# Splitting the output projection's weights and one group of down-projection weights ahead of their use in a hybrid decoder block

## The chip, the cores and the metric

One core of one Trainium2 chip runs the whole kernel. The metric is the device time of one execution in microseconds (us). The profile describes one execution by its span, from the first instruction to the end of the last; the time of that execution is a little longer than its span.

## What is computed

One decoder layer on a sequence of 2048 tokens with 1024 features, all in float32. An RMS norm, a combined input projection, two mixing branches (stick-breaking attention over 8 heads, chunked gated linear attention over 4 heads), an output projection with residual, a second norm, a convolutional feed-forward part with residual, and a last norm:

```python
h = rms_norm(x, attn_norm_g[l])
proj = h @ w_in[l]
...
x = x + jnp.concatenate([o_sb, o_gla], axis=-1) @ w_out[l]
h = rms_norm(x, ffn_norm_g[l])
u = causal_depthwise_conv(h @ w_ffn_up[l], conv_w[l], conv_b[l])
a, val = jnp.split(u, 2, axis=-1)
x = x + (jax.nn.silu(a) * val) @ w_ffn_down[l]
return rms_norm(x, final_norm_g)
```

`w_out` is 1024 x 1024, `w_ffn_down` is 2816 x 1024.

## The kernel before

**Split products.** Every large product is made of three matmuls. Each operand is split into a rounded high part and the remainder, and hi\*hi, hi\*lo and lo\*hi are added up in PSUM (lines 759 to 761 for the output and the down-projection). So each weight tile has to be split before it is used: `split_w` (line 101) copies it on ScalarE into the high part (L102) and subtracts on GpSimd, in a few places on VectorE, for the low part (L103). The 2048 tokens are worked on in four blocks of 512, and every block needs the same weights. Block 0 loads a weight raw (256 KB for 128 rows by 512 columns), splits it, uses it, and writes the split pair (512 KB) to a DRAM tile (`wou` for `w_out`, `wdn` for `w_ffn_down`, `wup` for the up-projection). Blocks 1 to 3 load the split pair. That choice stands in `load` (lines 741 to 752).

**Stages.** First, `prep` (line 193) normalises and transposes x, and `gv_block` (line 183) makes the values of the gated branch from it, 16 tiles of 128 tokens, in about 116 us. Then come the low-rank gate and the gated branch's queries and keys (lines 243 to 295), to about 220 us; the attention's Q, K and V projections together with the chunked linear attention (lines 416 to 430); the output gate together with the attention of block 0 (lines 650 to 679); and then, from about 680 us, four times `ffn` (line 812). `ffn` is the output projection (`accumulate`, line 728, once for each half n of the columns), the transposes, and three groups of 8, 7 and 7 chunks of up-projection, each followed by its share of the down-projection (`accumulate` again). The attention of blocks 1 to 3 is woven into the `ffn` stages.

**Buffers around the change.** `load_chunk` (line 148) loads the input projection's weights through the two `raw` buffers (line 125) and splits them into four `w` buffers. `m1` (line 128) is one buffer: it holds `gat` (the norm's gain) in the first stage, then `gvr` (the gated branch's values, line 300), and from line 708 on the split pair `d2`. In block 0 `accumulate` uses, for the first half of the output projection, raw tiles in slot 11 and four split pairs in slots 10 and 14 (`ahead`, lines 676 to 682); for everything else two raw tiles (`drr`) and a ring `dr` of three split pairs (lines 707 to 710). More pairs join `dr` only later (lines 724 to 725 and 926).

**What sets the order.** The program is unrolled. When it is built, a planner gives every engine and every DMA queue its order: it goes through the program with a timeline of its own, and lets an instruction that is ready by that timeline run ahead of earlier ones that are not (`schedule_with_timeline_sim=True`, line 992). On the chip each engine then runs its list in that order and waits on semaphores. From line 626 on TensorE alone keeps the order in which the program was written (`manual_schedule`). A tile of a pool with one buffer is only given out again when all that used it has finished, DMA included.

Of the kernel before, what the change touches and what calls it, by code (L numbers as in the profile page):

```python
# [8 lines left out]
F32 = mybir.dt.float32  # L9
# [7 lines left out]
P = 128  # L17
# [3 lines left out]
TB = 512  # L21
# [29 lines left out]
def hybrid_block_kernel(ctx, tc, x, attn_norm_g, w_in, w_gate_up, b_gate_up, sb_out_g,  # L51
# [66 lines left out]
    if True:  # L118
# [54 lines left out]
        def mm_tok(w, b, t):  # L173
            ps = mm_ps()
            whi, wlo = w
            ts = slice(t * P, (t + 1) * P)
            for k in range(KT):
                nc.tensor.matmul(ps, hh[b][k // 4][:, k % 4, ts], whi[k], start=(k == 0), stop=False)  # L178
                nc.tensor.matmul(ps, hh[b][k // 4][:, k % 4, ts], wlo[k], start=False, stop=False)  # L179
                nc.tensor.matmul(ps, hl[b][k // 4][:, k % 4, ts], whi[k], start=False, stop=(k == KT - 1))  # L180
            return ps

        def gv_block(w, b):
            for t in range(4):
                ps = mm_tok(w, b, t)
                gt = ev.tile([P, 2, TB], F32, tag="ev", name="gt")[:, 0]
                nc.scalar.activation(gt, ps, AF.Copy)
                nc.sync.dma_start(out=gvs[b][t * P:(t + 1) * P, :], in_=gt)

        with tc.tile_pool(name="xp", bufs=2, side="right") as xp, tc.tile_pool(name="sm", bufs=2, side="right") as sm:  # L190
            gat = m1_tile([P, D], F32, "gat")

            def prep(b):
                for t in range(4):
                    xt = xp.tile([P, D], F32, tag="xt", name="xt")
                    r0 = b * TB + t * P
                    nc.sync.dma_start(out=xt, in_=x[r0:r0 + P, :])
                    if r0 == 0:
                        nc.scalar.dma_start(out=gat, in_=attn_norm_g.to_broadcast([P, D]))
                    xn = xp.tile([P, D], F32, tag="xn", name="xn")  # L200
                    ss = sm.tile([P, 1], F32, tag="ss", name="ss")
                    nc.scalar.activation(xn, xt, AF.Square, accum_out=ss)
                    r = rstd_of(sm, ss, D, 1, "n")
                    nc.vector.scalar_tensor_tensor(out=xn, in0=xt, scalar=r, in1=gat, op0=ALU.mult, op1=ALU.mult)
                    for k4 in range(2):
                        tp = pt.tile([P, 4, P], F32, tag="tp", name="tp")
                        for kk in range(4):
                            k = 4 * k4 + kk
                            nc.tensor.transpose(tp[:, kk, :], xn[:, k * P:(k + 1) * P], ident)
                        dh = hh[b][k4][:, :, t * P:(t + 1) * P]  # L210
                        dl = hl[b][k4][:, :, t * P:(t + 1) * P]
                        split_psum(dh, dl, tp)

            prep(0)
            w = load_chunk(OFF_GV)
            for b in range(NB):
                if b + 1 < NB:
                    prep(b + 1)
                gv_block(w, b)
# [6 lines left out]
        with tc.tile_pool(name="lr", bufs=2, side="right") as lp, tc.tile_pool(name="lc", bufs=1, side="right") as lc:  # L226
# [16 lines left out]
            for b in range(NB):  # L243
                pl = mm_ps()
                for k in range(KT):
# [5 lines left out]
                nc.scalar.activation(lr[64:96, :], pl[0:32, :], AF.Copy)  # L251
                nc.vector.tensor_tensor(out=lr[32:64, :], in0=pl[0:32, :], in1=lr[0:32, :].bitcast(F32),
                                        op=ALU.subtract)
                pq0 = mm_feat(w, b, 0)
                for j in range(NPAIR):
                    pg = mm_ps()
# [397 lines left out]
    for b in range(NB):  # L654
        for t in range(4):
            for part, _ in enumerate(og_group(b, t)):
                if b > 0:

                    if steps < (16 * (b - 1) + 4 * t + part + 1) * FIRST // 46:
                        next(first, None)  # L660
                        steps += 1
                    for f, when in enumerate(PAIRS):
                        if f not in oT and steps >= when:
                            oT[f] = o_feat(0, f, pc, "c")
                for f, row in GATED.items():
                    if f not in oT and (b, t) >= row:
                        oT[f] = o_feat(0, f, pc, "c", ot=ots[f % 4])
            if (b, t) == (1, 3):
                gring.items += gated_rows(0)
                a4 = slot(4, [P, 4, TB], F32, "wtC")  # L670
                w45 = slot(5, [P, 2, 2, TB], F32R, "ws45")
                wsr.items += [w45[:, 0], w45[:, 1]]
                ots = [a4[:, k, :].rearrange("p (t q) -> p t q", t=4) for k in range(4)]
            elif (b, t) == (2, 3):
                gring.items += gated_rows(1)
                wraw = slot(11, [P, 4, TB], F32, "wraw")
                wsplit = slot(10, [P, 4, TB], F32R, "wsplit")
    for _ in first:
        pass
    wmore = slot(14, [P, 4, TB], F32R, "wmore")  # L680
    ahead = [Ring([wraw[:, k, :] for k in range(4)]),
             Ring([m[:, 2 * u:2 * u + 2, :] for m in (wsplit, wmore) for u in range(2)])]
    del wsr.items[2:]
    c1.close()
    rings, o2 = later_memory(*shared[:-1], a4, shared[-1])
# [39 lines left out]
            dr.items += [m[:, 2 * u:2 * u + 2, :] for m in spare for u in range(2)]  # L725
        return True

    def accumulate(lhs, w_rows, kept, b, squares=None, extra=None, stagger=False, rstds=None, rows=None, first=None,
                   final=False):


# [3 lines left out]
        for n in range(2):  # L735
# [4 lines left out]

            def load(ci):
                at_ = kept[n][rows[ci]]
                pair = first[1].next() if n == 0 and first else dr.next()
                if b > 0:
                    nc.sync.dma_start(out=pair.bitcast(F32), in_=at_.bitcast(F32))
                else:
                    raw = first[0].next() if n == 0 and first else drr.next()
                    nc.sync.dma_start(out=raw, in_=w_rows[rows[ci] * P:(rows[ci] + 1) * P, ns])
                    split_w(pair[:, 0, :], pair[:, 1, :], raw, nc.vector if first and n == 0 and ci % 2 else nc.gpsimd)
                    nc.gpsimd.dma_start(out=at_.bitcast(F32), in_=pair.bitcast(F32))  # L750
                whi, wlo = pair[:, 0, :], pair[:, 1, :]
                return whi, wlo
# [59 lines left out]
    def ffn(b, oT, rows, nextT):  # L812
# [15 lines left out]
        if b == 0:  # L828
# [4 lines left out]
        r2 = sm.tile([P, 4], F32, tag="r2", name="r2", bufs=2)  # L833
        rs1, rs2 = ([r[:, t:t + 1] for t in range(4)] for r in (r1, r2))
        last = b + 1 == NB
        yield from accumulate(oT, w_out, wou, b, squares=sq1, stagger=True, rstds=[r1], rows=rows,
                              extra=previous if b > 0 else remaining, first=None if b > 0 else ahead)
        if b == 0:
            h2h.extend(slot(10 + u, [P, 4, TB], F32R, f"h2h{u}") for u in range(2))
# [24 lines left out]
        for gi, G in enumerate(GROUPS):  # L864
# [49 lines left out]
            if final and b + 1 < NB:  # L914
                def extra(n, ci, G):
                    if ci == G - 1 or n == 1:
                        nextT.append(o_feat(b + 1, len(nextT), *((pc, "c") if done == total else (pz, "z"))))
            yield from accumulate(gts, w_ffn_down[ch0 * P:(ch0 + G) * P, :], [w[ch0:ch0 + G] for w in wdn], b, squares=sq2 if final else None,
                                  extra=extra, stagger=final and last, rstds=[r2], final=final and last)
            ch0 += G  # L920
        while b + 1 < NB and len(nextT) < KT:
# [74 lines left out]
```

## Time and profile before

| | us |
|---|---|
| median of 3 runs | 2766.29 |
| lowest and highest run | 2762.18, 2768.05 |
| time of the profiled execution | 2762.93 |
| its span | 2761.2 |

A row of the timeline reads: start and duration in us, engine, line, operation, the tile written and the tiles read, shapes, how many instructions were merged, and in square brackets how long the engine had been idle before and which event ended that idle time. PE is TensorE, DVE VectorE, ACT ScalarE, POOL GpSimd, SP the queue of SyncE; a DMA row gives the time to issue, not to transfer. In a table of windows each engine has its busy time and its count of instructions, followed by the TensorE clock that was granted (1.00 is 2.4 GHz, the lower level is 1.2 GHz, a value between them a mix of the two in time), the busy share of the DMA engines, and GB/s.

### The profile page before, as it was taken

Reading aid. Unit: us, or ns where it says so; the run is one execution under the profiler, and the core shown is the slowest. Engines: PE = TensorE matmul, PEld = TensorE weight load, DVE = VectorE, ACT = ScalarE, POOL = GpSimd, SP = SyncE. Lnnn points to the kernel's source line nnn. Section 1 sums busy time; section 2 is a strip of 40 time slices with the busy share of each in tenths; the row PEclk is TensorE's granted clock in tenths of the full one; section 3 lists DMA queues with packets and bytes.
Section 4 is the critical chain, followed back from the end, with each engine's and each line's share of the span. In section 5 each row is a group of like instructions: output and inputs, shape, how many; then the busy total and the mean of one; then the engine's idle time right before and its main releaser. Section 6 shows DMA issues by size and latency. Waiting matters only on the chain.

```text
span 2761.2 us, 36066 instructions
## 1 busy us (share of the span) xinstructions
PE 2696.3 (98%) x13000; PEld 2235.0 (81%) x13000; DVE 1686.7 (61%) x2777; ACT 1146.3 (42%) x2371; POOL 610.7 (22%) x937
## 2 busy tenths in 40 slices
PE   8999999999899899999999999999999999999998
PEld 7878888878688778887888888888888888888887
DVE  5246755457677687777776877777867334242333
ACT  5455533335465455554543444445434222220112
POOL 2001212214555555543111111111110000000000
PEclk9999999999999999999999999999999999999999
DMA  6215644477667677768455555574554656555552
GB/s 193 91 62 175 231 143 150 126 180 238 237 226 256 223 240 258 241 232 279 156 185 183 177 172 176 185 253 151 179 176 151 232 191 218 206 197 191 198 190 84
DMA packets 254563, 526.92 MB, mean 191 GB/s; under 512 B 54864, under 2 KB 143024, under 8 KB 231856
## 3 DMA queue, kind: packets, MB, share of 16 engines
q1 hardware_dynamic: 223136, 387.76, 42.8%
q0 software_dynamic: 31104, 136.33, 13.7%
q8 instruction: 102, 1.67, 0.2%
q14 instruction: 77, 0.63, 0.1%
q10 hardware_dynamic: 144, 0.52, 0.1%
HBM read 382.99 MB, written 141.56 MB: 190 GB/s over the span
## 4 chain that ended last, share of the span: by engine, by line
PE 85%; DVE 5%; DMA 4%; POOL 2%; ACT 2%; issue 2%; SPq 1%; ACTq 0%; POOLq 0%; DVEq 0%
PE ups L881 11%; PE ups L882 11%; PE ups L883 11%; PE d L760 6%; PE d L759 6%; PE d L761 6%; PE z L533 4%; PE tp L566 4%; PE mm L170 2%; PE mm L169 2%; PE mm L168 2%; PE acc L582 2%; PE mm L179 2%; PE mm L180 2%; PE mm L178 2%; PE acc L581 2%
## 5 line engine op out<-in xcount | busy, mean ns | idle before, releaser
L881 PE MATMUL ups<-h2h,u 128*128 128x512 f32 x1408 | 552.2, 392 | 3.9 <-DVE x L786 3.9
L882 PE MATMUL ups<-h2l,u 128*128 128x512 f32 x1408 | 551.0, 391 | 0.0
L883 PE MATMUL ups<-h2h,u 128*128 128x512 f32 x1408 | 550.3, 391 | 0.0
L881 PEld LDWEIGHTS ups<-h2h,u 128*128 128x128 f32 x1408 | 265.1, 188 | 60.5 <-DVE x L786 4.4
L883 PEld LDWEIGHTS ups<-h2h,u 128*128 128x128 f32 x1408 | 264.9, 188 | 57.2
L95 DVE TENSOR_TENSOR ws<-tp,ws 128x512 fp32r<-128x512 f32 (+1 forms) x320 | 193.8, 606 | 191.9 <-ACT ws L94 191.0
L882 PEld LDWEIGHTS ups<-h2l,u 128*128 128x128 f32 x1408 | 265.0, 188 | 55.5
L759 PE MATMUL d<-d,g 128*128 128x512 f32 x736 | 290.9, 395 | 4.2 <-DVE x L786 1.8
L94 ACT ACTIVATE ws<-tp 128x512 fp32r<-128x512 f32 (+1 forms) x320 | 170.2, 532 | 299.9 <-PE tp L566 295.5
L760 PE MATMUL d<-d,g 128*128 128x512 f32 x736 | 289.3, 393 | 1.5 <-POOL d L103 1.5
L761 PE MATMUL d<-d,g 128*128 128x512 f32 x736 | 288.7, 392 | 0.0
L893 DVE SCALAR_TENSOR_TENSOR ct<-ups,cwb,ct 128x511 f32<-128x511 f32 x176 | 131.7, 748 | 249.2 <-POOL ct L892 196.2
L888 ACT ACTIVATE ct<-ups,cwb 128x512 f32<-128x512 f32 x176 | 136.3, 775 | 340.3 <-PE ups L883 340.1
L549 DVE TENSOR_TENSOR_SCAN wtB<-mt,cy 128x512 f32<-128x512 f32 x192 | 248.4, 1294 | 3.1 <-ACT mt L538 3.0
L786 DVE TENSOR_TENSOR x<-d,x 128x512 f32<-128x512 f32 x128 | 85.8, 683 | 166.1 <-PE d L761 166.0
L892 POOL TENSOR_TENSOR ct<-ct,hadd 128x2 f32<-128x2 f32 x132 | 26.4, 200 | 688.7 <-ACT halo L890 324.5
L538 ACT ACTIVATE mt<-z 128x512 f32<-128x512 f32 (+2 forms) x320 | 170.5, 533 | 9.4 <-DVE cy L553 5.1
L759 PEld LDWEIGHTS d<-d,g 128*128 128x128 f32 x736 | 138.7, 189 | 36.0 <-DVE x L786 3.4
L760 PEld LDWEIGHTS d<-d,g 128*128 128x128 f32 x736 | 138.6, 188 | 31.8 <-POOL d L103 2.5
L761 PEld LDWEIGHTS d<-d,g 128*128 128x128 f32 x736 | 138.5, 188 | 30.9
L168 PE MATMUL mm<-hh,w 128*128 128x512 f32 x384 | 151.2, 394 | 0.0
L170 PE MATMUL mm<-hh,w 128*128 128x512 f32 x384 | 149.4, 392 | 0.8 <-POOL w L103 0.8
(262 smaller groups left out, 5375.4 us busy)
## 6 DMA issues: line engine op xcount, KB each, us to landing
u<-wup SPq DMA_DIRECT2D x132, 1024.0 KB, 4.7
d<-wdn SPq DMA_DIRECT2D x94, 512.0 KB, 3.4
wup<-u POOLq DMA_DIRECT2D x44, 1024.0 KB, 6.6
kvA<-kvs POOLq DMA_DIRECT2D x52, 512.0 KB, 4.8
uraw<-in_w_ffn_up_dram SPq DMA_DIRECT2D x44, 512.0 KB, 4.6
wdn<-d POOLq DMA_DIRECT2D x44, 512.0 KB, 5.2
d<-wou SPq DMA_DIRECT2D x38, 512.0 KB, 4.3
dw<-wdn SPq DMA_DIRECT2D x38, 512.0 KB, 4.2
```

Source lines behind the costliest of these rows:

```text
L94: nc.scalar.activation(hi, ps, AF.Copy)
L95: nc.vector.tensor_tensor(out=lo, in0=ps, in1=hi.bitcast(F32), op=ALU.subtract)
L168: nc.tensor.matmul(ps, whi[k][:, fs], hh[b][k // 4][:, k % 4, :], start=(k == 0), stop=False)
L170: nc.tensor.matmul(ps, wlo[k][:, fs], hh[b][k // 4][:, k % 4, :], start=False, stop=(k == KT - 1))
L538: nc.scalar.activation(m[:, lo:TB], z[:, :width], AF.Sigmoid, scale=-0.125)
L549: nc.vector.tensor_tensor_scan(out=pp[:, ::-1], data0=mr, data1=mr, initial=1.0 if prev is None else prev, op0=ALU.mult, op1=ALU.bypass)
L759: nc.tensor.matmul(accs[t], gh[:, ts], whi, start=(ci == 0), stop=False)
L760: nc.tensor.matmul(accs[t], gh[:, ts], wlo, start=False, stop=False)
L761: nc.tensor.matmul(accs[t], gw[:, ts], whi, start=False, stop=(ci == G - 1))
L881: nc.tensor.matmul(ps, whi[:, k, :], hk, start=(k == 0), stop=False)
L882: nc.tensor.matmul(ps, whi[:, k, :], lk, start=False, stop=False)
L883: nc.tensor.matmul(ps, wlo[:, k, :], hk, start=False, stop=(k == KT - 1))
```

## The change

A new helper loads a raw weight tile, splits it and writes the pair to DRAM. It is called 16 times in the first stage for all of `w_out`, through a pool `sp` with one raw tile and one pair, and 16 times in the second stage (four for each block) for the first 8 chunks of `w_ffn_down`, through the two `raw` buffers and the single `m1` buffer. Block 0 of the output projection, and the first group of block 0's down-projection, then load split pairs as the other blocks do. The first half of the output projection gets eight pairs (slots 10, 11, 14, 15) and needs no raw tiles.

```diff
+        def split_ahead(raw, pair, src, dst):
+            nc.sync.dma_start(out=raw, in_=src)
+            split_w(pair[:, 0, :], pair[:, 1, :], raw)
+            nc.gpsimd.dma_start(out=dst.bitcast(F32), in_=pair.bitcast(F32))
+
         def gv_block(w, b):
             for t in range(4):
+                i = 4 * b + t
+                split_ahead(sp.tile([P, 512], F32, tag="sraw", name="sraw"),
+                            sp.tile([P, 2, 512], F32R, tag="spair", name="spair"),
+                            w_out[(i // 2) * P:(i // 2 + 1) * P, (i % 2) * 512:(i % 2 + 1) * 512], wou[i % 2][i // 2])
                 ps = mm_tok(w, b, t)
...
+                tc.tile_pool(name="sp", bufs=1) as sp:
...
+                for i in range(4 * b, 4 * b + 4):
+                    split_ahead(raw_tile([P, 512], F32, "sraw"), m1_tile([P, 2, 512], F32R, "spair"),
+                                w_ffn_down[(i // 2) * P:(i // 2 + 1) * P, (i % 2) * 512:(i % 2 + 1) * 512],
+                                wdn[i % 2][i // 2])
                 pq0 = mm_feat(w, b, 0)
...
-                wraw = slot(11, [P, 4, TB], F32, "wraw")
-                wsplit = slot(10, [P, 4, TB], F32R, "wsplit")
+                wsplit = [slot(n, [P, 4, TB], F32R, f"ws{n}") for n in (10, 11)]
...
-    wmore = slot(14, [P, 4, TB], F32R, "wmore")
-    ahead = [Ring([wraw[:, k, :] for k in range(4)]),
-             Ring([m[:, 2 * u:2 * u + 2, :] for m in (wsplit, wmore) for u in range(2)])]
+    wsplit += [slot(n, [P, 4, TB], F32R, f"ws{n}") for n in (14, 15)]
+    ahead = Ring([m[:, 2 * u:2 * u + 2, :] for m in wsplit for u in range(2)])
...
-                pair = first[1].next() if n == 0 and first else dr.next()
-                if b > 0:
+                pair = first.next() if n == 0 and first else dr.next()
+                if split:
                     nc.sync.dma_start(out=pair.bitcast(F32), in_=at_.bitcast(F32))
                 else:
-                    raw = first[0].next() if n == 0 and first else drr.next()
+                    raw = drr.next()
                     nc.sync.dma_start(out=raw, in_=w_rows[rows[ci] * P:(rows[ci] + 1) * P, ns])
-                    split_w(pair[:, 0, :], pair[:, 1, :], raw, nc.vector if first and n == 0 and ci % 2 else nc.gpsimd)
+                    split_w(pair[:, 0, :], pair[:, 1, :], raw)
```

The output projection now passes `True` for `split`, the down-projection `b > 0 or gi == 0`.

## Rows read from the trace of the kernel before

**Rows 1.** The page, part 1: TensorE's busy time, share, instructions

```profile
PE 2696.3 (98%) x13000; PEld 2235.0 (81%) x13000; DVE 1686.7 (61%) x2777; ACT 1146.3 (42%) x2371; POOL 610.7 (22%) x937
```

**Rows 2.** Timeline of TensorE, 690 to 950 us, rows with idle time before

```profile
693.84 0.50 PE L760 MATMUL d<-wsplit,g 128*128 128x512 f32 x1 [0.88 <-POOL wsplit L103]
...
702.12 0.50 PE L759 MATMUL d<-wmore,g 128*128 128x512 f32 x1 [1.84 <-ACT wmore L102]
706.18 0.80 PE L760 MATMUL d<-wmore,g 128*128 128x512 f32 x1 [3.56 <-POOL wmore L103]
...
734.53 0.50 PE L759 MATMUL d<-d,g 128*128 128x512 f32 x1 [1.22 <-ACT d L102]
735.89 0.50 PE L760 MATMUL d<-d,g 128*128 128x512 f32 x1 [0.85 <-POOL d L103]
...
907.48 0.50 PE L581 MATMUL acc<-ws,kvA 128*128 128x512 f32 x1 [1.17 <-ACT ws L94]
...
947.57 0.50 PE L881 MATMUL ups<-h2h,u 128*128 128x512 f32 x1 [3.94 <-DVE x L786]
```

**Rows 3.** Windows of 10 us in block 0's output projection

```profile
700.00:710.00 10.00, 4.60 (x12) 3.24 (x11) 3.89 (x3) 3.12 (x5) 5.54 (x4) 0.66 1.05 405
...
730.00:740.00 10.00, 7.93 (x35) 6.23 (x34) 3.86 (x9) 4.26 (x10) 5.97 (x10) 0.86 0.93 308
```

**Rows 4.** The page, part 6: the SP queue's loads of split pairs

```profile
d<-wdn SPq DMA_DIRECT2D x94, 512.0 KB, 3.4
...
d<-wou SPq DMA_DIRECT2D x38, 512.0 KB, 4.3
```

**Rows 5.** Windows of 20 us in the first and the second stage

```profile
60.00:80.00 20.00, 20.00 (x106) 17.04 (x105) 10.11 (x12) 9.95 (x19) 3.28 (x8) 1.00 0.42 138
...
140.00:160.00 20.00, 20.00 (x90) 15.12 (x89) 6.72 (x11) 8.23 (x12) 0.19 (x1) 1.00 0.11 39
```

**Rows 6.** Timeline, 1069 to 1073 us: one split in block 0

```profile
1069.95 0.63 ACT L102 ACTIVATE d<-draw 128x512 fp32r<-128x512 f32 x1 [3.29 <-DMA draw<-in_w_ffn_down_dram]
1070.66 1.29 POOL L103 TENSOR_TENSOR d<-draw,d 128x512 fp32r<-128x512 f32 x1 [0.26 <-ACT d L102]
1072.25 0.57 POOL L750 DMA_DIRECT2D wdn<-d  x1 [0.30 <-POOL d L103]
```

**Rows 7.** The tile wdn in windows 880:920 and 920:960: its writes' time to landing

```profile
DMA to landing us min/median/max: 3.4/4.2/7.3
...
DMA to landing us min/median/max: 4.4/5.3/7.8
```

**Rows 8.** Timeline, 1224 to 1232 us: ScalarE waits for a pair's write

```profile
1224.80 1.11 POOL L750 DMA_DIRECT2D wdn<-d  x2
...
1227.93 0.60 PE L592 MATMUL tpf<-ident,wtB 128*128 128x128 f32 x4
...
1230.69 0.63 ACT L102 ACTIVATE d<-draw 128x512 fp32r<-128x512 f32 x1 [3.30 <-DMA wdn<-d]
1231.23 0.36 ACT L594 ACTIVATE ohp<-tpf 128x256 f32<-128x256 f32 x1
```

**Rows 9.** Timeline, 10 to 152 us: what the early stages have to spare

```profile
10.15 3.38 DVE L204 SCALAR_TENSOR_TENSOR xn<-xt,nr,gat 128x1024 f32<-128x1024 f32 x1 [0.72 <-POOL nr L89]
...
56.83 1.28 DVE L204 SCALAR_TENSOR_TENSOR xn<-xt,nr,gat 128x1024 f32<-128x1024 f32 x1
...
60.66 1.58 PE L209 MATMUL tp<-ident,xn 128*128 128x128 f32 x13
...
151.52 0.69 ACT L260 ACTIVATE e<-mm,bgate 128x512 f32<-128x512 f32 x1 [4.54 <-PE mm L257]
```

**Rows 10.** Timeline, 122 to 227 us: the raw buffers before the Q projection

```profile
122.75 1.65 SPq L152 DMA_DIRECT2D raw<-in_w_in_dram  x2
...
226.08 1.06 ACT L102 ACTIVATE w<-raw 128x1024 fp32r<-128x1024 f32 x1 [4.80 <-DMA raw<-in_w_in_dram]
```

**Rows 11.** Timeline of SP, 6 us: the low-rank gate's weights

```profile
6.20 1.28 SPq L228 DMA_DIRECT2D lraw<-in_w_in_dram  x1
```

More of the change, by code (lines that the diff above doesn't have):

```diff
@@ L188, in gv_block @@
                 nc.sync.dma_start(out=gvs[b][t * P:(t + 1) * P, :], in_=gt)
-        with tc.tile_pool(name="xp", bufs=2, side="right") as xp, tc.tile_pool(name="sm", bufs=2, side="right") as sm:
+        with tc.tile_pool(name="xp", bufs=2, side="right") as xp, tc.tile_pool(name="sm", bufs=2, side="right") as sm, \
+                tc.tile_pool(name="sp", bufs=1) as sp:
             gat = m1_tile([P, D], F32, "gat")
@@ L726, in after_attention, with accumulate @@
         return True
-    def accumulate(lhs, w_rows, kept, b, squares=None, extra=None, stagger=False, rstds=None, rows=None, first=None,
+    def accumulate(lhs, w_rows, kept, split, squares=None, extra=None, stagger=False, rstds=None, rows=None, first=None,
                    final=False):
@@ L835, in ffn @@
         last = b + 1 == NB
-        yield from accumulate(oT, w_out, wou, b, squares=sq1, stagger=True, rstds=[r1], rows=rows,
+        yield from accumulate(oT, w_out, wou, True, squares=sq1, stagger=True, rstds=[r1], rows=rows,
                               extra=previous if b > 0 else remaining, first=None if b > 0 else ahead)
@@ L917, in extra @@
                         nextT.append(o_feat(b + 1, len(nextT), *((pc, "c") if done == total else (pz, "z"))))
-            yield from accumulate(gts, w_ffn_down[ch0 * P:(ch0 + G) * P, :], [w[ch0:ch0 + G] for w in wdn], b, squares=sq2 if final else None,
+            yield from accumulate(gts, w_ffn_down[ch0 * P:(ch0 + G) * P, :], [w[ch0:ch0 + G] for w in wdn], b > 0 or gi == 0, squares=sq2 if final else None,
                                   extra=extra, stagger=final and last, rstds=[r2], final=final and last)
```

## The prediction

> **What bounds the kernel now.** I read the page first: TensorE is busy for 98% of the span [rows 1], so any work moved to another engine is worth only the gaps that it leaves in TensorE's row. Next I read TensorE's timeline where block 0 makes its own splits, and noted which engine ended each gap. Seven gaps between 690 and 950 us lead back to the splitting [rows 2]: five end with a high or low part that was not ready. The one at 907.48 ends with the attention's L94, which stood behind a split on ScalarE; the one at 947.57 ends with L786, whose four instructions stood on VectorE behind attention work that was itself behind a split whose raw tile had not landed. Then I read the windows around them: there the granted clock is 0.66 and 0.86, a mix of 2.4 and 1.2 GHz after the gaps [rows 3]. Last come the two early stages that take the work over: TensorE has no gap there, ScalarE works 10 and 8 us in 20, GpSimd next to nothing [rows 5].
>
> **What it removes.** The gaps of rows 2 add up to 0.88 + 1.84 + 3.56 + 1.22 + 0.85 + 1.17 + 3.94 = 13.5 us. The clock gives back (1 - 0.66) x 4.60 + (1 - 0.86) x 7.93 = 2.7 us [rows 3]. Together 16.1 us.
>
> **What block 0 pays instead.** A pair is now one load of 512 KB, 3.4 to 4.3 us from issue to landing [rows 4]. Eight pairs have buffers of their own in the first half of the output projection; four of these come free only after the output gate, but are needed 48 matmuls later, 10.7 us at 20.00 / 90 = 0.222 us each [rows 5]. That is hidden. The other three calls of `accumulate` still have a ring of three, and a load can't start before its buffer's last matmul. The fourth chunk's load starts when the first chunk is done and has one chunk, 12 x 0.222 = 2.7 us, to hide behind: 0.7 to 1.6 us late, three times. In the second half of the output projection the last three loads are wanted at once, with 6 matmuls (1.3 us) of cover: 2.1 to 3.0 us late. That is 4.2 to 7.8 us, or nothing where attention matmuls woven in between cover it. I take 4.2, since they cover some. The net gain is 16.1 - 4.2 = 11.9 us, between 8.3 and 16.1. The splits' writes are finished some 500 us before block 0 reads them, so it can't be that block 0 still waits for them.
>
> **What the early stages pay.** Engine time is there: 32 splits at 0.63 us on ScalarE and 1.29 + 0.57 us on GpSimd [rows 6], 20 and 60 us over 200 us, beside TensorE's work. GpSimd's subtraction can also hold VectorE up: the L204 that began with one running took 3.38 us instead of 1.28 [rows 9]; VectorE is half idle, so I cost that at nothing and let it widen the upper end. SP gets 32 more loads. The price is in the chain. `sp` and `m1` hold one pair each, so the next high part on ScalarE waits until the previous pair's write has landed. One turn is 0.63 + 0.08 + 1.29 + 0.30 [rows 6], some 0.1 us of signalling, and the landing: 2.4 us plus landing. Nothing else holds the 16 turns of a stage back, so the planner lets them run ahead, one after the other, at the turn that its timeline gives, with the stage's other ScalarE work in between. On the chip that order is fixed: if a write lands later than planned, all ScalarE work of the stage stands behind it, and the lags add up over 16 turns.
>
> How long does the planner think a write takes? ScalarE waited 3.30 us for a pair's write and began L102 at 1230.69; the two writes that can have been meant were issued at 1224.80 and about 1225.35, so they landed in 5.2 to 5.8 us. The L594 that stood behind had its input at 1227.93 + 0.60 = 1228.53 [rows 8]. The planner would have let it pass, had it expected the write later: it reckoned with at most 3.2 to 3.7 us. I take 3.2, the later write, hence a planned turn of at most 5.6 us and 16 x 5.6 = 90 us for the 16.
>
> First stage. The medians to landing are 4.2 and 5.3 us, the shortest 3.4 [rows 7]. The DMA engines are 0.42 busy at 138 GB/s [rows 5]; 768 KB more for each turn is some 120 GB/s on top, so I take 4.2, a window with such loads and writes. The lag is 16 x (4.2 - 3.2) = 16 us, of which the stage can take up 60.66 - 58.11 = 2.5 us, the time from the last L204 to its transposes [rows 9]: 13.5 us. At 3.4 us nothing is left; at 5.3 us it is 31.
>
> Second stage. The DMA engines are 0.11 busy [rows 5], so I take 3.8, between 3.4 and 4.2: 16 x 0.6 = 9.6 us, less the 4.5 us that ScalarE had to spare before L260 [rows 9], is 5.1 us; the ends are 0 and 11.5.
>
> The raw buffers. Q's first two raw tiles were issued at 122.75, some 96 us before use; now 16 small ones go first. The first lands at about 127, the fifteenth is split 14 x 6.2 + 2 us later, at 216, and Q's first raw tile lands at 220, the second at 226. The third had set the pace at 226.08 already [rows 10]. I take 2 us; the ends are 0 and 8. At the start the first item can push x's own work back by 0 to 1.9 us, its 0.63 + 1.29; I take 1.
>
> **Sum.** 13.5 + 5.1 + 2 + 1 - 11.9 = +9.7 us. The profiled execution took 2762.93 us, so 2772.6; it lies 3.4 below the median of 2766.29, so for a median I say **2776 us**. The ends are 2750 (all early work hidden, nothing late in block 0) and 2810 (31 + 11.5 + 8 + 1.9 - 8.3).
>
> The Trainium skill, DMA: Bandwidth & Descriptors, section "Anatomy of one DMA — SWDGE (gpsimd) path", puts a DMA issued by GpSimd at about 2.0 us plus its bytes over 436 GB/s, which gives an estimate of 3.2 us for 512 KB. With that the turn would be as planned, the lags would vanish, and the sum would be 2754. The 5.2 to 5.8 us of rows 8 and the medians of rows 7 speak for longer.
>
> **Rivals.**
> - Early work hidden. Faster: 2766.3 - 11.9 to 16.1, about 2753. It decides at a landing of 3.4 us or less while the early stages run, or at a planner that reckons with 4 us or more: then ScalarE never stands longer than it was meant to. For it: both stages have no gap on TensorE and half of ScalarE free, and 3.4 us does occur [rows 5, 7]. Against it: rows 8.
> - It evens out. One stage lags and the other doesn't, or the lag comes to about 12 us: 2761 to 2771, about 2766.
> - The pool `sp` takes memory which the low-rank gate's pool had. L228 loaded the gate's weights at 6.20 us [rows 11], long before its stage. If those 6 KB overlap, it can only start after the sixteenth write: with a first tile landed at about 8 us, at 8 + 16 x 6.6 = 114 us. It lands at 118 and is split by 120, when TensorE wants it at 116: some 4 to 10 us on top, about 2784.
>
> **How the numbers follow.** The forecast has 0.42, hidden work 0.36, evening out 0.15, the memory 0.07. A measurement tells 0.2%, 5.5 us, from no change. So faster is 0.36, the same 0.15, slower 0.42 + 0.07 = 0.49. The forecast's own range is 2771 to 2800. The range to hold 8 in 10 takes in hidden work and the forecast up to a lag of 30 us: 2750 to 2800.
>
> **What would show it.** Right: gaps on TensorE between 20 and 230 us, ended by transposes or L257 that go back to a ScalarE L102 waiting for a write to `wou` or `wdn`; the first stage ending some 13 us later than 116 us, the second some 20 later than 220; between 680 and 950 us the gaps of rows 2 gone, and new ones of 1 to 3 us at `accumulate`, ended by a DMA. Wrong: TensorE without gaps until 220 us. Then the planner's turn was long enough, and the time falls by what block 0 gains. If the gap at 947.57 stays, the gain is 4 us smaller.

## The result and the profile after

The change made the kernel slower: a median of 2797.16 us over 4 runs (2794.99 to 2799.19) against 2766.67 us for the kernel before beside it, a ratio of 1.0106 with a 95% interval of 1.0090 to 1.0122, some 29 us. The profiled execution took 2797.36 us, its span is 2795.7. From the new helper on, line numbers after are 10 to 15 higher than before.

I read TensorE's share first (the page, part 1), as in [rows 1]:

```profile
PE 2698.8 (97%) x13000; PEld 2237.4 (80%) x13000; DVE 1675.6 (60%) x2773; ACT 1147.3 (41%) x2371; POOL 622.4 (22%) x941
```

Busy time rose by 2.5 us, the span by 34.5: the loss is idle time. Next, TensorE's timeline of the kernel after, rows with idle time before them (in brackets: us idle, and what ended it):

```profile
149.68 0.64 PE L258 MATMUL mm<-hh,lw 128*32 128x512 f32 x1 [33.90 <-POOL lw L103]
...
189.22 0.50 PE L272 MATMUL mm<-lr,gu 96*128 96x512 f32 x1 [2.25 <-DVE lr L263]
...
202.91 0.50 PE L168 MATMUL mm<-hh,w 128*128 128x512 f32 x1 [1.94 <-DVE la L279]
...
232.25 0.68 PE L168 MATMUL mm<-hh,w 128*128 128x512 f32 x1 [2.88 <-DVE eb L303]
...
769.73 0.50 PE L772 MATMUL d<-d,g 128*128 128x512 f32 x1 [1.03 <-DMA d<-wou]
...
778.87 0.50 PE L772 MATMUL d<-d,g 128*128 128x512 f32 x1 [1.12 <-DMA d<-wou]
...
935.69 0.80 PE L772 MATMUL d<-d,g 128*128 128x512 f32 x1 [4.76 <-DMA d<-wdn]
```

One row is nearly as long as the whole loss: TensorE waits 33.9 us for the low-rank gate's weights `lw`. Three rows of 2 to 3 us follow in the second stage. In block 0 the gaps of [rows 2] are gone, and loads of split pairs end three new ones, 6.9 us together. The windows show the clock beside it, as in [rows 3, 5]:

```profile
60.00:80.00 20.00, 20.00 (x106) 17.05 (x105) 10.32 (x13) 11.11 (x21) 8.76 (x13) 1.00 0.61 199
120.00:140.00 20.00, 0.00 (x0) 0.00 (x0) 4.73 (x2) 4.20 (x6) 10.31 (x8) 0.50 0.64 209
140.00:160.00 20.00, 10.32 (x37) 6.32 (x38) 1.91 (x4) 4.04 (x8) 6.45 (x8) 0.65 0.46 154
180.00:200.00 20.00, 17.75 (x78) 13.75 (x77) 5.11 (x8) 7.53 (x12) 5.55 (x6) 1.00 0.44 157
...
760.00:770.00 10.00, 8.97 (x45) 7.49 (x44) 5.78 (x9) 4.20 (x11) 1.34 (x4) 1.00 0.43 150
770.00:780.00 10.00, 8.88 (x43) 7.10 (x43) 2.35 (x7) 1.15 (x3) 1.11 (x3) 1.00 0.63 218
```

In the first stage (60 to 80 us) TensorE is as full as before, although GpSimd works 8.76 us in place of 3.28. Between 120 and 140 us no matmul runs, the granted clock is at its lower level, 1.2 GHz, and it is still a mix (0.65) in the 20 us in which work starts again. In the two windows of the output projection it is at 1.00.

What is `lw` waiting for? I followed the four engines from the end of the early chain to that matmul (timeline, 137 to 150 us, in order of time):

```profile
137.82 0.63 ACT L102 ACTIVATE spair<-sraw 128x512 fp32r<-128x512 f32 x1 [3.80 <-DMA wou<-spair]
...
140.09 0.57 POOL L187 DMA_DIRECT2D wou<-spair  x1 [0.30 <-POOL spair L103]
...
143.21 0.48 DVE L251 MEMSET mask<- 128x512 f32 x1 [11.46 <-DMA wou<-spair]
...
143.39 0.38 SPq L239 DMA_DIRECT2D lraw<-in_w_in_dram  x1
...
147.24 0.63 ACT L102 ACTIVATE spair<-sraw 128x512 fp32r<-128x512 f32 x1 [5.84 <-DMA wdn<-spair]
147.77 0.29 ACT L102 ACTIVATE lw<-lraw 128x128 fp32r<-128x128 f32 x1
...
149.18 0.44 POOL L103 TENSOR_TENSOR lw<-lraw,lw 128x128 fp32r<-128x128 f32 x1
```

The sixteenth high part is made at 137.82, its write issued at 140.09. At 143.2, when that write has landed, two things start that have nothing to do with `w_out`: the memset of the gate's `mask` and the load `lraw` of the gate's weights, which before was issued at 6.20 us [rows 11]. Neither reads anything that the write made, so what they wait for is memory. The pool `sp` takes 6144 bytes of each partition (a raw tile of 2048 and a pair of 4096), the gate's `lraw`, `lw`, `gur`, `gu` and `mask` 5632, and the reading is that the second lie where the first lay; the first experiment tests it. By these rows, 27.4 us of the gap (115.8 to 143.2) are the wait for the pool's memory, and 6.5 us are the load, the split, and a ScalarE that stands 5.84 us behind a write to `wdn` in between.

The starts of matmuls of one kind mark the stages. A table of them, from the timelines of all profiled executions, is the base of what follows ("last Q/K": last matmul of the helper `mm_feat`; "up": first up-projection of block 0).

| kernel | low-rank: first | last | last Q/K | output projection | up | span |
|---|---|---|---|---|---|---|
| before | 115.9 | 197.2 | 433.8 | 681.7 | 764.5 | 2761.2 |
| after | 149.7 | 242.7 | 480.1 | 729.8 | 803.1 | 2795.7 |
| gate's tiles moved | 116.8 | 218.8 | 464.6 | 715.7 | 787.2 | 2783.3 |
| `w_out` ahead only | 152.4 | 234.9 | 471.5 | 720.2 | 796.5 | 2791.3 |
| `w_ffn_down` ahead only | 116.0 | 206.5 | 451.7 | 700.4 | 774.5 | 2772.5 |
| half-width pieces | 120.8 | 210.7 | 460.3 | 709.1 | 781.7 | 2774.3 |
| early work unused | 148.8 | 240.4 | 478.7 | 729.1 | 810.7 | 2808.2 |
| moved, `w_out` only | 116.9 | 205.9 | 444.1 | 694.6 | 769.5 | 2770.2 |
| the same, half-width | 117.6 | 201.5 | 439.1 | 688.9 | 765.1 | 2761.2 |
| moved, half-width, both | 119.1 | 213.5 | 450.1 | 700.7 | 771.8 | 2773.9 |
| `w_ffn_down` split, not written | 116.0 | 204.2 | 441.5 | 690.2 | 773.1 | 2765.7 |
| mask moved too | 118.9 | 201.2 | 439.1 | 690.2 | 766.1 | 2766.6 |
| two row tiles later | 118.2 | 200.7 | 438.7 | 688.5 | 764.8 | 2762.4 |
| a fourth pair | 119.2 | 201.6 | 439.3 | 689.9 | 762.7 | 2764.6 |

After against before: +33.8 at the first low-rank matmul, +11.7 to the last one, +0.8 to the last Q/K, +1.8 to the output projection; then -9.5 to the up-projection and -4.1 over the rest of the span. That sums to the 34.5 us of the spans. The rest after the up-projection is no firm number: it took 1996.7 us before, and in kernels that do the same work there 1996.1 (the same, half-width) and 2001.9 (a fourth pair). The table holds one execution of each kernel. That of the half-width `w_out` kernel was the fastest of its twelve runs, that of the kernel with `w_ffn_down` split but not written the fastest of its ten, and that of the kernel with a fourth pair the slowest of its nine.

### The profile page after: what moved, and what is told of

It is laid out like the page before. It is cut to its first block, busy times and chain, and to the rows that moved or that the text cites. A ratio compares the mean times of both kernels' runs of the same rounds, so it can differ in the third digit from the quotient of the medians.

```text
span 2795.7 us, 36128 instructions
## 1 busy us (share of the span) xinstructions
PE 2698.8 (97%) x13000; PEld 2237.4 (80%) x13000; DVE 1675.6 (60%) x2773; ACT 1147.3 (41%) x2371; POOL 622.4 (22%) x941
## 4 chain that ended last, share of the span: by engine, by line
PE 68%; DVE 3%; DMA 1%; ACT 0%; POOL 0%; issue 0%; ACTq 0%; POOLq 0%; DVEq 0%; SPq 0%
PE ups L894 11%; PE ups L895 11%; PE ups L896 11%; PE d L772 7%; PE d L773 7%; PE d L774 7%; PE z L548 4%; PE tp L581 4%; PE acc L597 2%; PE acc L596 2%; PE tpu L864 1%; DVE wtB L564 1%; DVE x L799 0%; DVE ohp L618 0%; DVE ws L95 0%; PE tpf L607 0%
## 5 line engine op out<-in xcount | busy, mean ns | idle before, releaser
L901 ACT ACTIVATE ct<-ups,cwb 128x512 f32<-128x512 f32 x176 | 136.4, 775 | 339.8 <-PE ups L896 339.5
```

## The experiments

Theory: the gate's tiles wait for the early pool's memory. Rivals: ScalarE is late in its own order; or the chain's length alone decides.

**The gate's tiles moved.** They get addresses outside the pool, in buffers that were taken to be idle there; nothing else changes.

```diff
-            lraw = lc.tile([P, KT, 16], F32, name="lraw")
+            lgr = n2_tile([P, 512], "lgr")
+            lraw = lgr[:, 0:128].rearrange("p (k r) -> p k r", r=16)
...
-            lw = lc.tile([P, KT, 2, 16], F32R, name="lw")
+            lw = low.tile([P, KT, 2, 16], F32R, tag="n", name="lw")
...
+            mg = ev.tile([P, 2, TB], F32, tag="ev", name="mg")
+            lrt = ev.tile([P, 2, TB], F32R, tag="ev", name="lrt")
...
-            mask = lc.tile([P, TB], F32, name="mask")
+            mask = mg[:, 0]
```

> The low-rank gate's tiles (raw weights, split weights, mask, low-rank rows) are moved to addresses that the early pool does not cover; all else is as in the changed kernel. Memory theory (the 33.9 us before the first low-rank matmul are the wait for the early pool's addresses to come free): the first low-rank matmul starts at 116 to 121 us in place of 149.7, the gap before it is under 6 us, and the time is about 2767 (2763 to 2773; the last four early writes now fall beside the low-rank work and may cost a few us there). Order theory (ScalarE is late in its own order because it stands behind the early writes): a gap of 20 us or more stays before the first low-rank matmul, and the time stays above 2785.

Measured: 2783.32 us, 1.0057 (1.0036 to 1.0077). The first low-rank matmul starts at 116.8, and no gap stands before it. The summary of that line, before and with moved tiles:

```profile
L247 PE MATMUL mm<-hh,lw x32: 391/397/398, 115.9 to 197.2; 128*32 128x512 f32 x32
```

```profile
L261 PE MATMUL mm<-hh,lw x32: 387/396/398, 116.8 to 218.8; 128*32 128x512 f32 x32
```

So the memory theory's mechanism is shown: the gap goes with the overlap. Its price is wrong: 14 us came back, not 30, and the time lies between the two forecasts. The last three pieces of `w_out` and the first three of `w_ffn_down`, which had been split during the gap, now run beside the low-rank work, and from the first low-rank matmul to the last Q/K it takes 347.8 us, 29.9 more than before. The order theory fell for the gap, but here its mechanism is at work. One such stall, with moved tiles (timelines of ScalarE, VectorE and TensorE, 200 to 208 us):

```profile
200.53 0.63 ACT L102 ACTIVATE spair<-sraw 128x512 fp32r<-128x512 f32 x1 [4.54 <-DMA wdn<-spair]
201.18 1.28 ACT L280 ACT_TABLE_LOAD   x1
202.48 0.72 ACT L280 ACTIVATE e<-e,one 128x512 f32<-128x512 f32 x1
...
203.23 0.69 DVE L283 TENSOR_TENSOR la<-la,e 128x512 f32<-128x512 f32 x1 [7.12 <-ACT e L280]
...
207.99 0.79 PE L168 MATMUL mm<-hh,w 128*128 128x512 f32 x1 [4.61 <-DVE la L282]
```

ScalarE stands 4.54 us before an early split, for the write that holds the only pair. The gate's own logarithm is behind it, VectorE has waited 7.12 us for that, and TensorE stops for 4.61 us. This is the mechanism of the prediction's forecast.

**`w_out` ahead only, and `w_ffn_down` ahead only.** The first leaves out the calls of the second stage, and block 0's first group splits for itself; the second leaves out the calls of the first stage with the pool, and the output projection splits for itself.

```diff
-                for i in range(4 * b, 4 * b + 4):
-                    split_ahead(raw_tile(...), m1_tile(...), w_ffn_down[...], wdn[i % 2][i // 2])
...
-            yield from accumulate(..., b > 0 or gi == 0, ...)
+            yield from accumulate(..., b > 0, ...)
```

```diff
-                split_ahead(sp.tile(...), sp.tile(...), w_out[...], wou[i % 2][i // 2])
...
-        yield from accumulate(oT, w_out, wou, True, ...)
+        yield from accumulate(oT, w_out, wou, b > 0, ...)
```

> Only the output projection's weights are split ahead; the down-projection's first group splits itself in the first block, as before the change. Theory that the down-projection's early work costs the second stage its own delay: the gap of about 34 us before the first low-rank matmul stays, the roughly 12 us lost between that matmul and the last low-rank one (and 2 us after it) go, the 4 us gained in the first block's first group go too, so about 2797 - 13 + 4 = 2788 (2784 to 2792). Rival (the delay inside the second stage is an after-effect of the stop of 34 us, such as the lower clock after it): the second stage stays as slow, and the time is about 2797 + 4 = 2801.

> Only the down-projection's first group is split ahead; the output projection splits its own weights, as before the change, and the early pool is gone. Theory of separate costs: no gap before the first low-rank matmul (116 us), about 12 us lost in the second stage and 2 after it, 4 gained in the first group, none of the 9.5 gained in the output projection: 2766.5 + 14 - 4 = 2776 (2772 to 2780). Rival (the second stage's delay only follows the stop before it): no delay there, 2766.5 - 4 = 2762.5.

Measured: 2791.70 us, 1.0080 (1.0057 to 1.0103), and 2777.33 us, 1.0031 (1.0015 to 1.0047). With `w_out` alone the gap is there (152.4), and from then to the last Q/K it takes 319.1 us, 1.2 more than before: the second stage's loss isn't an after-effect of the stop. With `w_ffn_down` alone there is no gap, and the same stretch takes 335.7 us, 17.8 more. The two costs are separate. Inside the first group nothing was gained: the wait of 3.94 us [rows 2] went, and this came in the kernel with `w_ffn_down` alone (TensorE's timeline):

```profile
906.75 0.79 PE L769 MATMUL d<-d,g 128*128 128x512 f32 x1 [4.52 <-DMA d<-wdn]
```

In the kernel after it is the 4.76 us at 935.69. The loads behind it land late there (the tile `d` in the window 900 to 940 us), in about twice the 3.4 to 4.3 us of [rows 4]:

```profile
DMA to landing us min/median/max: 7.2/7.5/9.4
```

But there is a gain ahead of the group, which [rows 2] doesn't list. Before, TensorE waits once in the transposes between the output projection and the up-projection:

```profile
754.90 3.17 PE L851 MATMUL tpu<-dg,x 128*128 128x128 f32 x26 [2.47 <-DVE dg L846]
```

The VectorE row that ends it took 1.50 us, with GpSimd splitting a piece of the first group beside it (L103 at 753.48); the other three of its kind took about 0.28. The prediction had seen such a hold-up [rows 9] and priced it at nothing. All nine kernels in which the first group splits for itself have this gap, 2.0 to 2.5 us; none of the five that load its pairs has it. In three pairs of kernels that differ in `w_ffn_down` alone, the stretch from the output projection to the up-projection is 3.0 us shorter with it ahead (73.3 after, 76.3 with `w_out` only), 3.4 (71.5, 74.9) and 5.1 (71.1, 76.2).

**Half-width pieces.** The pool keeps its 6 KB, as two raw pieces and two pairs of half the width; the gate's tiles stay under it.

```diff
-                split_ahead(sp.tile([P, 512], F32, tag="sraw", name="sraw"),
...
+                for c in range(2):
+                    split_ahead(sp.tile([P, 256], F32, tag="sraw", name="sraw"),
...
-                tc.tile_pool(name="sp", bufs=1) as sp:
+                tc.tile_pool(name="sp", bufs=2) as sp:
```

> The early pool works on pieces of half the width in two buffers of each kind (the same 6 KB of each partition); the low-rank tiles stay under it. Memory theory: the wait lasts until the last early write has landed, so it shortens with the chain: two writes in flight let a whole item pass in about 5 us instead of 8.3, the last write is issued near 118 us instead of 140, the first low-rank matmul starts at about 125 to 130 us, and the time is about 2773 to 2779. Rival (the chain is as long because each issue and split on GpSimd, now 32 of each, sets its pace): the first low-rank matmul stays at 145 us or later, and the time stays above 2790.

Measured: 2776.05 us, 1.0030 (1.0020 to 1.0040). TensorE's timeline:

```profile
120.79 0.42 PE L260 MATMUL mm<-hh,lw 128*32 128x512 f32 x1 [3.61 <-DMA gur<-in_w_gate_up_dram]
```

The time is as forecast, the first low-rank matmul starts even earlier than the 125 to 130 us expected. The gate's weights still wait under the pool, but the chain now ends with the first stage, and 33.9 us become 3.6. So the gap needs both, the overlap and a chain that outlasts the stage. The early writes of the kernel after and of this one (the tile `wou` up to 200 us; first and last start):

```profile
L187 POOL DMA_DIRECT2D wou<-spair x16: 571/600/782, 15.3 to 140.1; - x16
```

```profile
L187 POOL DMA_DIRECT2D wou<-spair x32: 682/698/886, 14.8 to 114.9; - x32
```

Twice as many writes end 25 us earlier. From the first low-rank matmul to the last Q/K it takes 339.5 us, 21.6 more than before; `w_ffn_down`'s part is unchanged here.

**The early work unused.** All early work stays; block 0 splits for itself as before the change, so its weights are written twice.

> All of the early work of the changed kernel stays, and nobody uses it: the first block loads raw weights and splits and writes them itself, as before the change (so its weights are written twice). Theory that the first block's gain is what the two traces show, 9.5 us in the output projection and 4 in the first group: 2797.2 + 13.5 = 2810.7 (2806 to 2815). Rival (the stalls of the output projection in the one execution before came from transfers that happened to collide, since the kernel with only the down-projection's part ahead also spent 8.7 us less there although it splits as before): the gain is nearer to 5, so 2802 (2799 to 2805).

Measured: 2809.51 us, 1.0146 (1.0120 to 1.0172). Against the ratio of the changed kernel that is 0.40%, 11 us, by which block 0 is faster for loading split pairs; the medians themselves differ by 12.4. The two intervals together leave that 11 us some 8 us of play either way. From the output projection to the up-projection it takes 81.6 us here, 73.3 after. The time lies in the theory's range and above the rival's; by the intervals alone a gain of 5 isn't excluded. Traces speak against it too: of the four kernels that split the output projection's weights in block 0, three take 82.8 us (before), 81.6 (here) and 82.9 (`w_ffn_down` split, not written) for this stretch. Only the kernel with `w_ffn_down` alone, on which the rival rests, took 74.1 in the profiled execution. Of the 8.7 us between it and the kernel before, 2.5 are the gap in the transposes that it doesn't have. The other difference that stands out is one SP row, the same load of a raw tile, before and with `w_ffn_down` alone:

```profile
690.91 5.83 SPq L748 DMA_DIRECT2D draw<-in_w_out_dram  x1
```

```profile
709.64 1.95 SPq L758 DMA_DIRECT2D draw<-in_w_out_dram  x1
```

In the two other kernels this row takes 4.55 and 6.83 us. Whether 1.95 belongs to that kernel or to that execution, one trace doesn't tell.

**`w_out` only, gate's tiles moved; the same in half-width pieces; both weights in half-width pieces.** The first two join edits above. The third adds half-width pieces for `w_ffn_down`, with raw buffers of their own:

```diff
+                if b == 0:
+                    m12 = m1_tile([P, 2, 2, 256], F32R, "spair")
...
-                    split_ahead(raw_tile([P, 512], F32, "sraw"), m1_tile([P, 2, 512], F32R, "spair"),
...
+                    for c in range(2):
+                        split_ahead(mg[:, 1, c * 256:(c + 1) * 256], m12[:, c],
```

> Low-rank tiles moved out from under the early pool, and only the output projection's weights split ahead, in one full-width pair. The first low-rank matmul starts at 116 to 118 us. Theory that the second stage's loss of 30 us with moved tiles is mostly the down-projection's work: what is left of the early chain after 116 us costs up to 5, the gain of the output projection is 5 to 9.5, so 2762 (2757 to 2767). Rival (the last early writes, now between the second stage's instructions on ScalarE, cost the 12 us by which the moved kernel lost more there than the kernel with the down-projection's part alone): 2766.5 + 12 - 9 = 2770 or more.

> As the run before, with the early chain in half-width pieces and two buffers, so that it ends with the first stage. Theory: neither stage loses more than 2 us, the output projection gains 5 to 9.5, so 2759 (2756 to 2763), faster than both kernels. Rival (the gain is hidden, the output projection's stalls being those of colliding transfers): within 2 us of the kernel before.

> Both parts split ahead, low-rank tiles moved, both chains in half-width pieces with two buffers, and the down-projection's raw pieces in buffers of their own. Theory that the second stage's loss is ScalarE's wait for the write of a single pair: with two pieces in flight the 18 us that the kernel with the down-projection's part alone lost there shrink to 8 or less, so about 2764 (2759 to 2769). Rival (the loss is the work itself: 16 splits more on in-order queues, and their traffic beside the loads of the next weights): 18 us stay, so about 2775 (2771 to 2780).

Measured: 2770.94 us, 1.0015 (1.0001 to 1.0030); 2769.52 us, 1.0007 (0.9991 to 1.0024); 2773.05 us, 1.0014 (0.9998 to 1.0029). None is faster. In full width the time lies at the rival's value. In half width the forecast of 2759 fails and the time is the rival's, but not for the rival's reason: the stretch from the output projection to the up-projection gains 6.6 us (76.2 in place of 82.8), but it starts 7.2 us late. My own edit made part of that, in full width too. VectorE's timeline with half-width pieces:

```profile
125.83 0.48 DVE L256 MEMSET mg<- 128x512 f32 x1 [5.12 <-DMA gvs<-gt]
126.34 0.68 DVE L268 TENSOR_TENSOR lrt<-mm,lrt 32x512 fp32r<-32x512 f32 x1
```

The mask had moved onto a buffer that the first stage's last write still held, and the low-rank result stood behind its memset: the same fault as the change's, 5 us long (in full width the wait is 4.53 us, so that the rival isn't borne out by its time alone). The kernel with the gate's tiles moved has it too, so a small part of its 29.9 us is this edit and not the change. TensorE's timeline there:

```profile
134.68 0.79 PE L275 MATMUL mm<-lrt 96*128 96x512 f32 x1 [1.60 <-DVE lrt L266]
```

With both weights, the stretch to the last Q/K takes 331.0 us, 13.1 more than before. But the half-width kernel without `w_ffn_down` already takes 321.5, so `w_ffn_down`'s part is 9.5. Between the two full-width kernels with moved tiles it is 347.8 - 327.2 = 20.6. By these traces two pieces in flight, with raw buffers of their own, halve the loss. That is close to the theory's 8, and the rival's 18 doesn't hold, although the time, 2773.05, lies in the rival's range and not in the theory's.

**`w_ffn_down` split early, but not written.** The kernel with `w_ffn_down` alone, without the early write; the first group splits for itself.

```diff
             split_w(pair[:, 0, :], pair[:, 1, :], raw)
-            nc.gpsimd.dma_start(out=dst.bitcast(F32), in_=pair.bitcast(F32))
```

> The kernel with the down-projection's part alone, but its early pieces are only loaded and split, never written to DRAM, and the first group splits for itself in the first block as before the change (the result is the same as before; the early splits are useless work). Theory that the 18 us lost between the first low-rank matmul and the last query and key matmul are waits for the write, which hold ScalarE's other work back: without the write the span between those two matmuls is within 4 us of the 317.9 before, and the time is 2767 to 2772. Rival (the splits themselves and the loads beside them cost it): the span stays 12 or more longer, and the time is 2779 or more.

Measured: 2771.86 us, 1.0018 (1.0004 to 1.0031). The stretch takes 325.5 us, 7.6 more than before, between the two forecasts; the time is in the theory's range. Of the 17.8 us, 10.2 go with the write, 7.6 with the splits and loads themselves, by one trace of each. ScalarE's waits before an early high part from 116 to 250 us, with the write, then without it (total us, times, longest):

```profile
ACT spair L102 <- issue: 22.4, 7, 4.7
ACT spair L102 <- DMA wdn<-spair: 17.8, 5, 6.5
```

```profile
ACT spair L102 <- DMA sraw<-in_w_ffn_down_dram: 12.1, 8, 2.8
```

The first row is time for which the profile names no cause; without the write there is no such row. So with the write ScalarE stands some 40 us before the early pieces, without it 12.1 us for the raw pieces and little else. How the 7.6 divide between ScalarE's order and GpSimd was not tried.

**Towards a better version.** Three steps from the half-width kernel with `w_out` only: the mask and the raw gate weights into `m1`, which is free after the norm's gain when no piece of `w_ffn_down` uses it; the early pieces two row tiles later in the program; and a fourth pair for the second half of the output projection, in the memory of the raw tiles that it no longer needs (they get it back after the output projection).

```diff
+            mg = m1_tile([P, 2, TB], F32, "mg")
```

```diff
+                s = 4 * b + t
+                for h in range(32 * max(s - 2, 0) // 14, 32 * max(s - 1, 0) // 14):
+                    i, c = h // 2, h % 2
```

```diff
-    drr = Ring([drt[:, 0, :], drt[:, 1, :]])
+    dr.items.append(wd.tile([P, 2, 512], F32R, tag="draw", name="dpre", bufs=1))
+    drr = Ring([])
```

> Only the output projection's weights ahead, early chain in half-width pieces with two buffers, low-rank tiles moved, and now the mask and the raw low-rank weights in memory that is free at 85 us (the run with moved tiles and half-width pieces lost 2.5 us where the mask's memset waited for the last write of the first stage). Theory: that wait goes, the low-rank matmuls end within 2 us of before, so 2 to 4 us less than that run: 2766 (2762 to 2769), at best 0.2% below before. Rival (its loss ahead of the first block is ScalarE's and the queues' use in the first stage): no change from that run's 2769.5.

> As the run before, but the early pieces begin two row tiles later, so that the first transposes, where the run with half-width pieces lost 1.7 us, have ScalarE and GpSimd to themselves. Theory: 1 to 2 us less than the run before, 2764 (2760 to 2768). Rival (the denser pieces then push the chain past the end of the first stage): 2 to 4 us more than the run before, through a wait before the first low-rank matmuls.

> As the run with the early pieces two row tiles later, and the output projection's second half loads into four pairs in place of three (the fourth is the raw buffer, which nobody needs there when no weights are split). Theory: the two waits of about 0.8 and 1.2 us that end with a load of the split weights go, so 2 us less, 2762 (2758 to 2766), 0.2% below before. Rival (the loads are late because SP issues them late, behind the loads of the up-projection's weights): the waits stay and the time does not change.

Measured: 2765.94 us, 0.9988 (0.9974 to 1.0002); 2764.30 us, 0.9992 (0.9978 to 1.0006); 2759.51 us over 9 runs, 0.9974 (0.9960 to 0.9988). The first two are close to what was expected, and too small to tell from no change. In the second, the later place in the program changed nothing that it was meant to: the first early write starts at 14.8 us there, 14.7 in the first, since the planner let it run ahead all the same; whether a later start helps stays open. The third is faster than the kernel before by 0.26%, some 7 us (0.12 to 0.40%). What it removed are these rows of TensorE's timeline of the kernel without the fourth pair:

```profile
726.73 0.49 PE L773 MATMUL d<-d,g 128*128 128x512 f32 x1 [0.83 <-DMA d<-wou]
...
736.00 0.50 PE L773 MATMUL d<-d,g 128*128 128x512 f32 x1 [1.25 <-DMA d<-wou]
```

The loads themselves, by SP's timeline without and with the fourth pair:

```profile
721.99 10.84 SPq L759 DMA_DIRECT2D d<-wou  x5
```

```profile
723.55 3.73 SPq L759 DMA_DIRECT2D d<-wou  x3
730.32 0.32 SPq L759 DMA_DIRECT2D dpre<-wou  x1
```

Without it five loads in a row share a ring of three buffers and are issued over 10.84 us; with it three are out after 3.73 us, and one more, at 730.32, goes to the fourth buffer. No gap of 0.5 us or more on TensorE ends with a load of `wou` between 690 and 780 us there, so the theory holds. From the output projection to the up-projection it takes 72.8 us, 10.0 less than before, but the output projection starts 8.2 us late. That makes 1.8 us in the trace, of its slowest run, against 7 by the medians; where the other 5 us lie isn't shown.

## Why the prediction was right and wrong

The sign was right and 2797 lies in the range, but that is luck as far as the sum goes: its largest term was nothing, 2776 was 21 us short, and the loss came from a place that had a chance of 0.07.

- **Gain in block 0, 11.9 us: right in total, its terms not.** 11 to 12.4 by the runs, with the play given above. The gaps of [rows 2] and the low clock went, 16.1 us, and a gap of 2.47 us that the prediction's count of seven had left out. The new load waits were 1.03 + 1.12 + 4.76 = 6.9 us in place of 4.2, near the upper bound of 7.8. The largest was priced at 0.7 to 1.6 us, from loads that land in 3.4 to 4.3; they took 7.2 to 9.4. So 16.1 + 2.5 - 6.9 = 11.7 us: two errors that cancel.
- **First-stage lag, 13.5 us: wrong, it was nothing.** The last of the first stage's value matmuls starts at 115.4 us, 115.6 before. The step that failed is "the planner lets them run ahead, one after the other" at 5.6 us a turn. From the first high part at 12.98 to the sixteenth at 137.82 the mean turn is 124.84 / 15 = 8.3 us, and while x was being prepared it was about one piece for each tile of finished values (8 pieces and 9 such tiles on ScalarE before 77 us). The writes did land as I took them, if anything later (the tile `wou` in the windows 0 to 60 and 60 to 145 us):

```profile
DMA to landing us min/median/max: 4.4/5.0/5.5
...
DMA to landing us min/median/max: 2.9/4.4/6.3
```

  But with the pieces this far apart there was room: in the first 60 us ScalarE waited for them 2.4 us in all. The 31.4 us of such waits came between 60 and 145 us, mostly after x's transposes were through at 82, with nothing of the first stage behind them but copies of finished values. So in this stage the lags vanished, though not because the writes were quick. The Trainium skill's figures for a DMA issued by GpSimd (DMA: Bandwidth & Descriptors, section "Anatomy of one DMA — SWDGE (gpsimd) path") give an estimate of 3.2 us for such a write; both medians here are longer. (The prediction's sum by that estimate, 2754, also drops its own 2 and 1 us for the raw buffers and the start; with them it is 2757.)
- **The pool under the gate's tiles, 4 to 10 us: the right mechanism, mis-sized.** It cost 33.9 us. The price had the sixteenth write landed at 114 us, at 6.6 us a turn, and the gate's weights split by 120. In fact that write was issued at 140.09 and landed by 143.2, and the weights were split at 149.6. The long turn that made the first stage harmless is what made the overlap dear. The chance was too low as well: the profile held the load at 6.20 us [rows 11], and the pools' sizes stood in the program.
- **Second stage and raw buffers, 5.1 + 2 us: the right mechanism, too small.** By itself the work costs 17.8 us here; the kernel after shows only 11.7 + 0.8, since part of the work fell into the gap of 33.9 us. Of the 17.8, 10.2 go with the write, within the ends of 0 to 11.5; the 7.6 of the splits and loads themselves had been taken as hidden.
- **Start, 1 us:** no such loss; the first stage ends 0.2 us earlier.
- **Rivals:** hidden work was true of the first stage alone. Evening out did not happen; it is about what moving the tiles and halving the pieces bring (1.0014).

## What to carry to other kernels

When a pool is put where another one was, ask whose memory it takes and when that one's first load used to start: a load that looked free at 6 us becomes the last link of somebody else's chain. Work moved to engines with time to spare can cost more by its place in their order than by its duration: 16 splits of 0.63 us on ScalarE, and what goes with them, cost TensorE 17.8 us. Count which later instruction stands behind each wait, and give a write-back chain two buffers, if need be of half the size. And weigh the gain by what the moved work still costs where it now stands: here 10.0 us gained in block 0 stood against 8.2 us lost ahead of it in the best version's trace, with half of the change taken out and the rest repaired, and its medians gained 7.

## What was not expected of the hardware

The same SP load of 256 KB held its queue for 5.83, 4.55 and 6.83 us in three kernels and 1.95 in a fourth, one execution each, with the DMA share above 1.0 every time; the fourth lost some 5 us less around it. Loads of split pairs, 3.4 to 4.3 us by the medians of the execution before [rows 4], took 7.2 to 9.4 us in one window of block 0 after the change (DMA share 0.61 to 0.87). After 33.9 us without a matmul, the first low-rank matmul took 0.64 us in place of the usual 397 ns, and the granted clock was 0.50 and then 0.65 over the 40 us around.
